# SBUF byte addresses of the split operands in a two-layer fp32 encoder step

## The chip, the cores and the metric

The kernel runs on one core of one Trainium2 chip. The metric is the device time of one execution in microseconds (us), given as the median of several runs. A profile of one execution comes with it: for every instruction its engine, its start, its duration and what it waited for. Times of single instructions are in ns. The engines are PE (matrix multiply), PEld (the weight loads that go with it), DVE, ACT and POOL (element work) and SP, whose queue issues most of the DMAs.

## What is computed

One inference step of a small two-layer encoder, over 1024 new rows and 64 rows of a running stream (1088 columns in the kernel, which works on transposed data). Cut to what matters here:

```python
def swiglu(u, w_in, w_out):
    g, up = jnp.split(u @ w_in, 2, axis=-1)
    return (jax.nn.silu(g) * up) @ w_out

def reference(...):
    for layer in range(2):
        nw = norm_w[layer]
        if layer == 0:
            mp, hp, cp = ssd_mixer(rmsnorm(xp, nw[0]), h0, c0, *params)
            ms, hs, cs = ssd_mixer(rmsnorm(xs, nw[0]), state_ssm[0], state_conv[0], *params)
        else:
            kp, vp = shared_kv(xp, kv_norm_w, w_kv)
            ks, vs = shared_kv(xs, kv_norm_w, w_kv)
            mp = prompt_band_attention((rmsnorm(xp, nw[0]) @ w_q), kp, vp, rel_bias) @ w_o
            ms = sample_band_attention((rmsnorm(xs, nw[0]) @ w_q), ks, vs, cache_k, cache_v, rel_bias) @ w_o
        xp = xp + rmsnorm(mp, nw[1])
        xs = xs + rmsnorm(ms, nw[1])
        xp = xp + rmsnorm(swiglu(rmsnorm(xp, nw[2]), ffn_w_in[layer], ffn_w_out[layer]), nw[3])
        xs = xs + rmsnorm(swiglu(rmsnorm(xs, nw[2]), ffn_w_in[layer], ffn_w_out[layer]), nw[3])
```

Model width is 1024, the hidden width of the feed-forward part 2816 (22 tiles of 128), the mixer's inner width 2048. Everything is float32.

## The kernel before, in words

**Split products.** Every large matrix product is made of three PE matmuls. Both operands are split into a high part, rounded to PE's `float32r` type, and the rest: weights into `h` and `l_`, activations into `xh` and `xl`. The three products are `h*xh`, `h*xl` and `l_*xh` (lines 458 to 460 in `passes`, 1304 to 1306 in `run_pair`, 1503 to 1505 in the second feed-forward product). In each matmul the weights, 128 by 128, are loaded into PE and stay there while the activations, 128 rows by 256 to 384 columns, stream past them. The weights are loaded anew for each matmul.

**Tiles in SBUF.** A tile is a block of bytes that has the same address in all 128 partitions. The tiles that this case is about:

- `r`, 16 tiles of 4608 bytes in pool `rp`: split activations of the mixer and of the attention, and in the feed-forward part those of the second half of the columns.
- `rx`, 13 tiles of 4096 bytes in pools `rx0` and `rx1`, one pool for each layer's back part: split activations of the first 512 columns, later part of the hidden activations; some are lent as landing places for weights from DRAM (`Lent`).
- `hl`, 3 tiles of 8192 bytes: the split weights. `hx`, 2 more of them at the start of each back part. `half` (split) and `tt` (unsplit): parts of weights for the seven-product scheme of `run_pair`.
- `raw`: weights as they come from DRAM. `sg`: landing places for hidden activations. `p1`, `u2`, `u3`, `c22`, `x` in pool `tm`: results of `run_pair` on their way to the gate.

Activations in `r` and `rx` lie there in blocks of 256, 288, 320 or 384 columns of 4 bytes, weights in blocks of 128 columns. All of these are multiples of 128 bytes, so each operand of a split matmul begins at the same byte in 128 as its tile.

**Order.** PE's instructions are recorded in the order of the code (`manual_schedule`); the class `Stream` puts side tasks between them by a clock of its own. The other engines are ordered by a scheduler with priorities. `Weights` loads and splits weights ahead of their use: DMA into `raw` or a lent `rx` tile, ACT rounds to the high part (line 340), DVE subtracts (line 341).

**Stages on the profile's time axis.** Mixer up to about 640 us; its output projection (`project`, 256 and 288 columns) to about 850; back part of layer 0, with `plain_pairs` (256 columns) to 920, `run_pair` (256 columns from `rx`, 288 from `r`) to 1327 and the second product (384, 384 and 320 columns) to about 1570; attention to about 2075; its output projection; and from about 2200 the back part of layer 1, built in the same way.

**Where addresses come from.** Pools are laid out one behind the other in the order in which they are opened, tiles in a pool likewise, each rounded up to 32 bytes. So the byte at which a tile begins follows from the sizes of all that lie before it.

Of the kernel before, what the change touches and what calls it, by code (L numbers as in the profile page):

```python
# [8 lines left out]
F32 = mybir.dt.float32  # L9
# [7 lines left out]
P = 128  # L17
# [120 lines left out]
class Ring:  # L138
# [9 lines left out]
    def get(self):  # L148
        assert self.free(), self.tag
        self.live += 1  # L150
        return self.pool.tile(self.shape, self.dtype, tag=self.tag, bufs=self.bufs, name=self.tag)
# [55 lines left out]
class Lent:  # L207
# [7 lines left out]

    def get(self):
        self.live += 1
        return self.ring.get()

    def put(self):  # L220
        self.live -= 1
# [153 lines left out]
def hybrid_kernel(  # L375
# [9 lines left out]
    def pool(es, name, bufs=1, **kw):  # L385
        return es.enter_context(tc.tile_pool(reuse_waits="tile", name=name, bufs=bufs, **kw))

    cp = pool(ctx, "cp")
    dr = ctx.enter_context(tc.tile_pool(name="dr", bufs=1, space=DRAM))
    wp = pool(ctx, "wp")  # L390
    rp = pool(ctx, "rp")
    nsb = pool(ctx, "nsb")
    pmm = pool(ctx, "pmm", 2, space=PSUM)
    pax = pool(ctx, "pax", 2, space=PSUM)
# [20 lines left out]
    yTv = yT_o.rearrange("(t p) n -> p t n", p=P)  # L415

    R = Ring(rp, "r", NR, [P, 1152])
    RX = Ring(None, "rx", 0, [P, 1024])
    W = Weights(
        nc, Ring(wp, "raw", RAWB, [P, 1024]), Ring(wp, "hl", HLB, [P, 2, 1024], F32R),  # L420
        Ring(None, "half", 0, [P, 2, 512], F32R), Ring(None, "tt", 0, [P, 1024]),
    )
    W.tc, W.lent = tc, Lent(RX)
    W.raws.append(W.lent)
# [13 lines left out]
    def ax(name):  # L438
        if side[0] and name in ("nst", "nbp"):
            return side[0].tile([P, 512], F32, tag="yy", name=name)  # L440
        return pax.tile([P, 512], F32, tag="ax", name=name)
# [44 lines left out]
    def rstd(ssum, inv, r, nb, more=None):  # L486

        sp = ax("nst")
        if more is None:
            for i in range(nb):  # L490
                PE.transpose(sp[:, i * P:(i + 1) * P], ssum[:, i * P:(i + 1) * P], ident)
        else:
            for j, t in enumerate((ssum, more)):
                for i in range(nb):
                    c = 4 * j + i
                    PE.matmul(sp[:, c:c + 1], t[:, i * P:(i + 1) * P], ones[:, 0:1], start=True, stop=True)
        with tc.high_priority(HIP):
            v = nsb.tile([P, 12], F32, tag="nv", bufs=2, name="nv")
            a, h, y = v[:, 0:nb], v[:, 4:4 + nb], v[:, 8:8 + nb]
            if more is None:  # L500
                sums = sp[:, :nb * P].rearrange("p (a b) -> p a b", b=P)
                V.tensor_reduce(a, sums, axis=mybir.AxisListType.X, op=ALU.add)
                V.tensor_scalar(a, a, inv, EPS, op0=ALU.mult, op1=ALU.add)
            else:
                V.tensor_scalar(a, sp[:, :nb], inv, EPS, op0=ALU.mult, op1=ALU.add)
                V.scalar_tensor_tensor(a, sp[:, 4:4 + nb], inv, a, op0=ALU.mult, op1=ALU.add)
            V.tensor_scalar(y.bitcast(I32), a.bitcast(I32), -0.5, float(0x5F3759DF), op0=ALU.mult, op1=ALU.add)


            V.tensor_tensor(h, y, y, op=ALU.mult)  # L510
            V.tensor_tensor(h, h, a, op=ALU.mult)
            V.scalar_tensor_tensor(a, h, RP[0], h, op0=ALU.add, op1=ALU.mult)
            V.scalar_tensor_tensor(a, a, RP[1], h, op0=ALU.add, op1=ALU.mult)
            V.scalar_tensor_tensor(a, a, RP[2], h, op0=ALU.add, op1=ALU.mult)
            V.scalar_tensor_tensor(r, a, RP[3], y, op0=ALU.add, op1=ALU.mult)

    def bcast(r, a, n, rb=None):

        bp = ax("nbp")
        for i in range((a + n + P - 1) // P):  # L520
            PE.transpose(bp[:, i * P:(i + 1) * P], r[:, i:i + 1].to_broadcast([P, P]), ident)
        if rb is None:
            rb = nsb.tile([P, 384], F32, tag="rb", bufs=1, name="rb")
        A.activation(rb[:, :n], bp[:, a:a + n], AF.Copy, scale=RL)
        return rb[:, :n]

    def rb_steps(ssum, n, out, wait=None, rb=None, more=None):

        nb = (n + P - 1) // P
        nr = nsb.tile([P, 4], F32, tag="nr", bufs=2, name="nr")  # L530
        rstd(ssum, 1.0 / D, nr[:, :nb], nb, more)
        yield 0.3, wait or RB_WAIT
        with tc.high_priority(HIP):
            out.append(bcast(nr, 0, n, rb))
        yield 0.35, 0
# [121 lines left out]
    with ExitStack() as es:  # L657
# [413 lines left out]
        for s in range(NSL):  # L1071
            us, n = u[s], SL[s][1]
            pl, tg = pyy, "yy"
# [68 lines left out]
    def op_build(ops, done, when=lambda: True):  # L1142


        n, qa, qb = ops.n, 2 * ops.b, 2 * ops.b + 1
        rings = (RX, R) if ops.b == 0 else (R,)
        L, rg = {}, {}
# [64 lines left out]
    def chain(layer, q, y, ss, cw, xsrc, xout, cpre, done):  # L1212

        o, n = QS[q]

        rings = (RX, R) if q < 2 else (R,)
        w_post, w_rb, w_pre = CHW[layer][q // 2]
# [43 lines left out]
    def plain_pairs(ts, ops, hd, px, tmp):  # L1261

        n = ops.n
        first = ts == PGS[0]
        xs, ws = {}, {}
        for t_, i, q in [(t_, i, q) for t_ in ts for i, q in (((0, 0), (1, 0), (0, 1), (1, 1)) if first else ((0, 0), (0, 1), (1, 0), (1, 1)))]:
            if (t_, i) not in ws:
                ws[t_, i] = W.get()
            st.wait_for(lambda: all(a_ in ops.plain for a_ in (f"a{q + 1}1", f"a{q + 1}2")))
            uq = ops.plain[f"a{q + 1}1"] + ops.plain[f"a{q + 1}2"]  # L1270
            if i == 0:
                xs[t_, q] = tmp.tile([P, n], F32, tag=("p1", "u3")[q] + f"{t_ % 2}", name="x")
            x = xs[t_, q]

            def gate(ps):
                with tc.high_priority(HIP):
                    A.activation(x, ps[:, :n], AF.Silu)

            def mult(ps):
                with tc.high_priority(HIP):  # L1280
                    V.tensor_tensor(x, ps[:, :n], x, op=ALU.mult)  # L1281
                nc.sync.dma_start(hd[:, t_, q * n:(q + 1) * n], x)

            unit(ws[t_, i], uq, n, mult if i else gate, pl=px)
            if q:
                W.put()
# [58 lines left out]
    def back(layer, start, cpost, xsrc, xmid, cpre, cpost2, xout, rb_out, done2):  # L1345
# [3 lines left out]
        with ExitStack() as es:  # L1349
            px = pool(es, f"px{layer}", 4, space=PSUM)  # L1350
            RX.pool, RX.bufs = pool(es, f"rx{layer}"), NRX
            sgp = pool(es, f"sg{layer}")
            stage[0] = lambda: sgp.tile([P, 384], F32, tag="sg", bufs=SGB, name="sg")

            def loader():

                for s, (o, n) in enumerate(SL):
                    yield 0, 0, lambda: phase[0] > (s > 0)
                    cells = Cells(n, *(((RX, 99), (R, 8)), ((R, 9), (RX, 99)), ((RX, 99), (R, 3)))[s])
                    for k in range(FT):  # L1360
# [10 lines left out]
            def end_load(s):  # L1371
                o, n = SL[s]
                xc = Cells(n, (R, 99)) if s == 2 else Cells(n, (RX, 99), (R, 99))
                yield 0, EP_W[s] if s < 2 else 0, lambda: xc.room(KD)
# [78 lines left out]
            with ExitStack() as e2:  # L1453
                tmp = pool(e2, f"tm{layer}")
                e3 = ExitStack()
                W.hx.pool, W.hx.bufs = pool(e3, f"hx{layer}"), 2
                W.advance()
                ops[0].yring, ops[1].yring = RX, R
                start(ops, px, lambda q, y, ss: st.spawn(chain(layer, q, y, ss, cpost, xsrc, xmid, cpre, dn)), dn)
                for ts in PGS:  # L1460
                    if ts == PGS[1]:
                        W.hx.bufs = 0
                    elif ts == PGS[-1]:
                        assert W.hx.live == 0
                        e3.close()
                        W.tt.pool, W.tt.bufs = pool(e2, f"tt{layer}"), 2
                        W.half.pool, W.half.bufs = W.tt.pool, 2

                        W.pri = HIP
                        W.advance()  # L1470
                    plain_pairs(ts, ops[0], hd, px, tmp)
                for r in ops[0].rings["a21"]:
                    r.put()
                for t_, bs, ends in [(t_, (0, 1), (0,) if t_ == FT - 1 else ()) for t_ in range(NB0, FT)] + [(t_, (1,), (1,) if t_ == NB0 - 1 else ()) for t_ in range(NB0)]:
                    run_pair(t_, W.get(), bs, ends, ops, hd, px, tmp, t_ == NB0)
                    W.pri = 0
                    if t_ == FT - 1:
                        phase[0] = 1
                        W.lent.cap = 2
                        st.spawn(loader())  # L1480
                W.tt.bufs = W.half.bufs = 0
# [5 lines left out]
            for s, (o, n) in enumerate(SL):  # L1487
# [3 lines left out]
                for m in range(KD):  # L1491
# [3 lines left out]
                    for k0, nk in KCH:  # L1495
                        w = W.get()
                        h, v = w["w"]
# [47 lines left out]
    rba = [rbp.tile([P, 384], F32, tag=f"rbf{s}", name="rbf") for s in range(NSL)]  # L1545
    done2 = []
    back(0, start_ssd, nwc(0, 1), xTv, x1d, nwc(0, 2), nwc(0, 3), x2d, rba, done2)


# [384 lines left out]
    def start_att(ops, px, after, dn):  # L1934
# [14 lines left out]
        st.spawn(op_build(ops[1], dn))  # L1949

    back(1, start_att, nwc(1, 1), x2d, x3d, nwc(1, 2), nwc(1, 3), yTv, None, [])
    st.flush()
    yY.close()
# [96 lines left out]
```

## Time and profile before

| what | value |
|---|---|
| median of 3 runs | 2952.55 us (2948.33 to 2952.82) |
| the profiled execution's own time | 2953.14 us |
| its span, first to last instruction | 2951.4 us |
| granted PE clock over the span | 0.997 |
| instructions | 56260, of them 21562 matmuls |

How to read it: the span is the stretch between the first and the last instruction; the 1.7 us between it and the execution's own time lie around it. In the groups of the profile a matmul's row names its line, the PSUM tile it writes, the tiles that it reads (`mmx<-r,hl` reads an `r` and an `hl` tile), the shape of the streamed operand, the count, the sum in us and the mean in ns. Matmuls are pipelined: the next one starts long before the one before has ended, so the mean duration is longer than the distance from start to start. `mm` and `mmx` are the PSUM tiles of `unit`, `px` those of `run_pair`, `po` that of the second feed-forward product.

### The profile page before, as it was taken

What the parts mean: (1) busy time and instruction counts of PE and PEld (TensorE: products, weight loads), DVE (VectorE), ACT (ScalarE), POOL (GpSimd) and SP (SyncE); (2) the same over time, 40 slices, a digit from 0 to 9 for tenths busy, and PEclk for the clock granted to TensorE, in tenths of its full rate; (3) what the DMA queues carried; (4) which work ended last, traced back from release to release, by engine and by line L of the source; (5) the groups of instructions that cost most, each with busy time, mean ns of one, the idle gap of its engine ahead of it and who ended that gap; (6) DMA issues with size and microseconds to landing.
All of it is one profiled execution on the core that took longest, in us unless ns stands there. A gap on an engine that the chain in (4) does not pass through costs nothing.

```text
span 2951.4 us, 56260 instructions
## 1 busy us (share of the span) xinstructions
PE 2911.9 (99%) x21562; PEld 2871.3 (97%) x21562; DVE 2032.0 (69%) x4452; ACT 1402.8 (48%) x2531; POOL 728.2 (25%) x884
## 2 busy tenths in 40 slices
PE   8999999999999999999999999999999999999999
PEld 8999999999999999999999899999999999999999
DVE  7887878885867545583567787778688555575544
ACT  6655546454443222353445665556664322244443
POOL 1333333331022434351111000000131434351111
PEclk9999999999999999999999999999999999999999
DMA  4333333335564222345665322223375222245754
GB/s 138 124 99 100 109 100 106 100 120 164 158 191 118 76 84 73 108 152 163 205 190 158 88 79 71 64 69 105 127 201 173 78 84 72 83 151 173 226 172 136
DMA packets 202846, 368.07 MB, mean 125 GB/s; under 512 B 20688, under 2 KB 149424, under 8 KB 202576
## 3 DMA queue, kind: packets, MB, share of 16 engines
q1 hardware_dynamic: 199920, 354.97, 38.3%
q0 software_dynamic: 2656, 9.51, 1.8%
q8 instruction: 169, 2.77, 0.4%
q14 instruction: 101, 0.83, 0.1%
HBM read 297.19 MB, written 62.74 MB: 122 GB/s over the span
## 4 chain that ended last, share of the span: by engine, by line
PE 86%; DVE 7%; DMA 3%; ACT 2%; issue 1%; POOL 0%; SPq 0%; DVEq 0%; ACTq 0%; POOLq 0%
PE px L1304 9%; PE px L1305 9%; PE px L1306 9%; PE mm L458 7%; PE mm L460 7%; PE mm L459 7%; PE po L1504 6%; PE po L1505 6%; PE po L1503 6%; PE mmx L460 3%; PE mmx L459 3%; PE mmx L458 3%; PE ptp L1736 2%; PE po L1771 2%; PE S L1705 1%
## 5 line engine op out<-in xcount | busy, mean ns | idle before, releaser
L458 PE MATMUL mm<-r,hl 128*128 128x384 f32 (+2 forms) x1704 | 565.5, 332 | 3.2 <-DVE craw L740 1.0
L460 PE MATMUL mm<-r,hl 128*128 128x384 f32 (+2 forms) x1704 | 549.9, 323 | 4.3 <-DVE hl L353 2.9
L459 PE MATMUL mm<-r,hl 128*128 128x384 f32 (+2 forms) x1704 | 548.5, 322 | 0.0
L341 DVE TENSOR_TENSOR hl<-raw,hl 128x1024 fp32r<-128x1024 f32 x216 | 255.6, 1184 | 217.8 <-ACT hl L340 215.6
L1305 PE MATMUL px<-r,hl 128*128 128x288 f32 (+1 forms) x1184 | 347.3, 293 | 0.0
L458 PEld LDWEIGHTS mm<-r,hl 128*128 128x128 f32 x1704 | 322.2, 189 | 6.0 <-DVE craw L740 1.1
L460 PEld LDWEIGHTS mm<-r,hl 128*128 128x128 f32 x1704 | 321.5, 189 | 6.2 <-DVE hl L353 4.2
L459 PEld LDWEIGHTS mm<-r,hl 128*128 128x128 f32 x1704 | 322.2, 189 | 0.3
L1304 PE MATMUL px<-r,hl 128*128 128x288 f32 x1056 | 311.0, 295 | 0.0
L1306 PE MATMUL px<-r,hl 128*128 128x288 f32 x1056 | 310.7, 294 | 0.0
L340 ACT CAST hl<-raw 128x1024 fp32r<-128x1024 f32 x216 | 216.9, 1004 | 161.5 <-PE po L1505 102.3
L484 POOL TENSOR_TENSOR ssum<-ssum,sq 128x256 f32<-128x256 f32 (+3 forms) x97 | 127.1, 1311 | 617.3 <-ACT sq L483 601.9
L1305 PEld LDWEIGHTS px<-r,hl 128*128 128x128 f32 x1184 | 222.3, 188 | 0.0
L1306 PE MATMUL px<-rx,hl 128*128 128x256 f32 x768 | 215.0, 280 | 5.2 <-DVE hl L341 5.2
L1304 PE MATMUL px<-rx,hl 128*128 128x256 f32 x768 | 215.6, 281 | 1.7 <-DVE x L1281 1.7
L1504 PE MATMUL po<-rx,hl 128*128 128x384 f32 (+1 forms) x624 | 201.7, 323 | 0.7 <-DVE rx L1368 0.7
L1304 PEld LDWEIGHTS px<-r,hl 128*128 128x128 f32 x1056 | 198.4, 188 | 0.4 <-DVE u L1319 0.4
L1306 PEld LDWEIGHTS px<-r,hl 128*128 128x128 f32 x1056 | 198.3, 188 | 0.0
L1503 PE MATMUL po<-rx,hl 128*128 128x384 f32 (+1 forms) x608 | 197.3, 324 | 0.0
L1505 PE MATMUL po<-rx,hl 128*128 128x384 f32 (+1 forms) x608 | 196.5, 323 | 0.0
L1305 PE MATMUL px<-rx,hl 128*128 128x256 f32 x640 | 178.8, 279 | 0.0
L1306 PEld LDWEIGHTS px<-rx,hl 128*128 128x128 f32 x768 | 145.3, 189 | 5.9 <-DVE hl L341 5.9
(364 smaller groups left out, 7921.7 us busy)
## 6 DMA issues: line engine op xcount, KB each, us to landing
raw<-in_w_f_dram SPq DMA_DIRECT2D x154, 512.0 KB, 3.8
rx<-in_w_f_dram SPq DMA_DIRECT2D x54, 512.0 KB, 3.6
raw<-in_w_in_dram SPq DMA_DIRECT2D x40, 512.0 KB, 3.6
MT<-ascr SPq DMA_DIRECT2D x48, 384.0 KB, 4.3
sg<-hscr SPq DMA_DIRECT2D x88, 192.0 KB, 3.6
raw<-in_w_f_dram SPq DMA_DIRECT2D x44, 384.0 KB, 3.3
raw<-in_w_so_dram SPq DMA_DIRECT2D x32, 512.0 KB, 3.8
raw<-in_w_o_dram SPq DMA_DIRECT2D x19, 512.0 KB, 3.7
```

The costliest lines, as they stand in the source:

```text
L340: self.nc.scalar.copy(h, v)
L341: (eng or self.eng or self.nc.vector).tensor_tensor(lo, v, h, op=ALU.subtract)
L458: PE.matmul(ps[:, :n], h_, xh, start=(first and i == 0), stop=False)
L459: PE.matmul(ps[:, :n], h_, xl, start=False, stop=False)
L460: PE.matmul(ps[:, :n], l_, xh, start=False, stop=(last and i == nk - 1))
L484: (eng or G).tensor_tensor(ssum[:, :n], ssum[:, :n], q[:, :n], op=ALU.add)
L1304: PE.matmul(ps, wh, ah[:, k, :], start=(k == 0), stop=False)
L1305: PE.matmul(ps, wh, al[:, k, :], start=False, stop=False)
L1306: PE.matmul(ps, wl, ah[:, k, :], start=False, stop=(k == 3))
L1503: PE.matmul(ps[:, :n], wh, xh, start=(k == 0), stop=False)
L1504: PE.matmul(ps[:, :n], wh, xl, start=False, stop=False)
L1505: PE.matmul(ps[:, :n], wl, xh, start=False, stop=(k == FT - 1))
```

## The change

No instruction is added, removed or moved: on all five engines the sequences of instructions are the same but for the numbers of buffers. Of the waits two differ: one ACT copy of 256 columns into an `rx` tile waits for one more DMA queue, and one POOL memset of a `K` tile no longer waits for PE. What changes is where tiles lie:

```diff
     def get(self):
         self.live += 1
-        return self.ring.get()
+        return self.ring.get()[:, :1024]
...
     wp = pool(ctx, "wp")
+    nss = pool(ctx, "nss")
     rp = pool(ctx, "rp")
+
+    def shift(pl):
+        pl.tile([P, 16], F32, name="shift")
+
     nsb = pool(ctx, "nsb")
...
-    RX = Ring(None, "rx", 0, [P, 1024])
+    RX = Ring(None, "rx", 0, [P, 1028])
...
-            v = nsb.tile([P, 12], F32, tag="nv", bufs=2, name="nv")
+            v = nss.tile([P, 12], F32, tag="nv", bufs=2, name="nv")
...
-        nr = nsb.tile([P, 4], F32, tag="nr", bufs=2, name="nr")
+        nr = nss.tile([P, 4], F32, tag="nr", bufs=2, name="nr")
...
                 W.hx.pool, W.hx.bufs = pool(e3, f"hx{layer}"), 2
+                shift(W.hx.pool)
...
                         W.tt.pool, W.tt.bufs = pool(e2, f"tt{layer}"), 2
+                        shift(W.tt.pool)
```

The small tiles `nv` and `nr` (192 bytes with rounding) move from behind `r` to a pool of their own ahead of it, so `r` begins 192 bytes later. The `rx` tiles grow by 16 bytes, which rounding makes 32. The first byte of each tile in 128, as the two programs are built:

| tile | before | after |
|---|---|---|
| `r` | 32 | 96 |
| `rx` | 96 | 96, 0, 32, 64 in turn |
| `hl`, `raw` | 32 | 32 |
| `hx`, `half`, `tt` | 96 | 64 |
| `sg`, tiles of pool `tm` | 96 | 0 |
| `ssum`, `sq` | 32 | 96 |
| tiles of the mixer and of the attention (`K`, `Qh`, `Ql`, `Vn` and others) | 64 or 96 | the same |

So the distance from the weights to the activations, (activations minus weights) in 128, changes as follows. The counts are split matmuls in the program.

| columns | activations on weights | matmuls | distance before | distance after |
|---|---|---|---|---|
| 256 | `r` on `hl` | 1364 | 0 | 64 |
| 256 | `r` on `hx` | 204 | 64 | 32 |
| 256 | `rx` on `hl` | 2860 | 64 | 64 (996), 96 (612), 0 (600), 32 (652) |
| 256 | `rx` on `half` | 384 | 0 | 64 (256), 96 (128) |
| 256 | `rx` on `hx` | 180 | 0 | 64 (60), 96 (40), 32 (60), 0 (20) |
| 288 | `r` on `hl` | 3792 | 0 | 64 |
| 288 | `r` on `half` and `hx` | 1056 | 64 | 32 |
| 320 | `r` on `hl` | 1760 | 0 | 64 |
| 320 | `rx` on `hl` | 832 | 64 | 64 (232), 96 (176), 0 (192), 32 (232) |
| 384 | `r` on `hl` | 4176 | 0 | 64 |
| 384 | `rx` on `hl` | 1008 | 64 | 64 (336), 96 (96), 0 (288), 32 (288) |

Of the 2860 matmuls of `rx` on `hl`, the 600 that come to distance 0 are 152 into `mmx` and 448 into `px`; the 1264 that come to 96 or 32 are 304 into `mmx` and 960 into `px`.

## The prediction

> **What bounds the kernel now.** I read the page first: busy time of each engine, then the chain that ended last.
>
> ```profile
> span 2951.4 us, 56260 instructions
> ...
> PE 2911.9 (99%) x21562; PEld 2871.3 (97%) x21562; DVE 2032.0 (69%) x4452; ACT 1402.8 (48%) x2531; POOL 728.2 (25%) x884
> ...
> PE 86%; DVE 7%; DMA 3%; ACT 2%; issue 1%; POOL 0%; SPq 0%; DVEq 0%; ACTq 0%; POOLq 0%
> ```
>
> PE is busy for 2911.9 of 2951.4 us and makes 86% of the chain. What PE saves or loses per matmul goes almost whole into the time, if addresses change a matmul at all. So I next read the groups by shape, for the same line and the same number of columns with other tiles.
>
> ```profile
> L458 PE MATMUL mmx<-rx,hl 128*128 128x256 f32 x228 | 64.4, 282 | 0.0
> L459 PE MATMUL mmx<-rx,hl 128*128 128x256 f32 x228 | 63.2, 277 | 0.0
> L460 PE MATMUL mmx<-rx,hl 128*128 128x256 f32 x228 | 63.1, 277 | 0.0
> L458 PE MATMUL mmx<-r,hl 128*128 128x256 f32 x220 | 62.5, 284 | 0.6 <-ACT r L602 0.6
> L460 PE MATMUL mmx<-r,hl 128*128 128x256 f32 x220 | 62.3, 283 | 1.1 <-DVE hl L341 1.1
> ...
> L459 PE MATMUL mmx<-r,hl 128*128 128x256 f32 x220 | 62.2, 283 | 0.5 <-DVE r L603 0.5
> ...
> L459 PE MATMUL mmx<-r,hx 128*128 128x256 f32 x68 | 18.8, 277 | 0.0
> ...
> L459 PE MATMUL mmx<-rx,hx 128*128 128x256 f32 x60 | 17.0, 283 | 0.0
> ...
> L1706 PE MATMUL S<-K,Ql 128*128 128x256 f32 x16 | 4.2, 280 | 0.0
> ```
>
> Set beside the table of distances: `rx` on `hl` and `r` on `hx`, distance 64, take 277. `r` on `hl` and `rx` on `hx`, distance 0, take 283. Each activation tile and each weight tile stands once on either side, so neither `r` nor `hx` is slow by itself; the pair is. `K` on `Ql`, distance 0 too, has 280. These durations hold a pipeline latency, so I checked the starts in the timeline (columns: start in us, duration), in a steady stretch of each.
>
> ```profile
> 2135.24 0.28 PE L460 MATMUL mmx<-r,hl 128*128 128x256 f32 x1
> ...
> 2136.92 0.28 PE L459 MATMUL mmx<-r,hl 128*128 128x256 f32 x1
> ```
>
> ```profile
> 2256.78 0.28 PE L460 MATMUL mmx<-rx,hl 128*128 128x256 f32 x1
> ...
> 2257.57 0.28 PE L458 MATMUL mmx<-rx,hl 128*128 128x256 f32 x1
> ```
>
> 14 steps in 1.68 us are 120 ns from start to start at distance 0; 7 steps in 0.79 us are 113 at distance 64. The difference is really time on PE. With more columns there is none:
>
> ```profile
> L1305 PE MATMUL px<-r,hl 128*128 128x288 f32 x1056 | 311.4, 295 | 0.0
> ...
> L1504 PE MATMUL po<-r,hl 128*128 128x384 f32 x368 | 123.1, 335 | 0.0
> ...
> L1504 PE MATMUL po<-rx,hl 128*128 128x384 f32 x336 | 112.6, 335 | 0.0
> ...
> L1505 PE MATMUL po<-rx,hl 128*128 128x320 f32 x272 | 83.9, 308 | 0.0
> ...
> L1305 PE MATMUL px<-r,half 128*128 128x288 f32 x176 | 51.9, 295 | 0.0
> ...
> L1505 PE MATMUL po<-r,hl 128*128 128x320 f32 x80 | 24.7, 309 | 0.0
> ...
> L1706 PE MATMUL S<-K,Ql 128*128 128x512 f32 x16 | 6.3, 392 | 0.0
> ```
>
> At 288 columns distance 0 and 64 both take 295, at 384 both 335, at 320 it is 309 against 308. The weight loads tell why:
>
> ```profile
> L459 PEld LDWEIGHTS mmx<-rx,hl 128*128 128x128 f32 x228 | 42.9, 188 | 0.0
> ...
> L459 PEld LDWEIGHTS mmx<-rx,hx 128*128 128x128 f32 x60 | 11.5, 191 | 0.0
> L746 PEld LDWEIGHTS dtp<-r,dtw 128*64 128x64 f32 x24 | 3.2, 135 | 0.7
> ```
>
> A load of 64 weight columns takes 135, one of 128 takes 188: 53 for 64 columns, so about 107 of the 188 are reading. That is nearly the whole 113 of a 256-column matmul: there the load of the next weights sets the pace, and at distance 0 it is itself longer (191). A stream of 288 columns or more outlasts the load and hides it.
>
> **The change part by part.** Prices are per matmul, distance 0 against 64, at 256 columns.
>
> In `mm` and `mmx` the means of the three lines give 283.3 against 278.7, so 4.7; the steady starts give 7. I take 6. In `px` the pieces are short and alternate with 288 columns:
>
> ```profile
> L1304 PE MATMUL px<-rx,hl 128*128 128x256 f32 x768 | 215.6, 281 | 1.7 <-DVE x L1281 1.7
> L1306 PE MATMUL px<-rx,hl 128*128 128x256 f32 x768 | 215.0, 280 | 5.2 <-DVE hl L341 5.2
> L1305 PE MATMUL px<-rx,hl 128*128 128x256 f32 x640 | 178.8, 279 | 0.0
> ...
> L1304 PE MATMUL px<-rx,half 128*128 128x256 f32 x128 | 36.2, 283 | 0.8 <-DVE p L1321 0.8
> L1306 PE MATMUL px<-rx,half 128*128 128x256 f32 x128 | 36.2, 283 | 0.0
> L1305 PE MATMUL px<-rx,half 128*128 128x256 f32 x128 | 36.1, 282 | 0.0
> ```
>
> 282.7 against 280: 2.7.
>
> `r` to byte 96. 1364 matmuls on `hl` go from distance 0 to 64, a pairing of bytes (96 on 32) that `rx` on `hl` has now: 1364 x 6 ns = 8.2 us less. The 9728 of 288, 320 and 384 columns on `hl` go the same way; the rows above say 0 within 1 ns, so nothing, with 5 us either way if half of that ns is real.
>
> `rx` in turn. 600 on `hl` come to distance 0: 152 x 6 + 448 x 2.7 = 2.1 us more. On `half` and `hx`, now at byte 64, 256 x 2.7 + 60 x 6 = 1.1 us less.
>
> The distances 32 and 96 have no row at 256 columns. Bounds: like 64, the 128 + 100 matmuls that leave distance 0 save 128 x 2.7 + 100 x 6 = 0.9 us and all others stay; like 0, the 960 + 304 of `rx` on `hl` and 204 of `r` on `hx` cost 960 x 2.7 + 508 x 6 = 5.6 us. The nearest row is `dtw` (byte 64, 384 columns from byte 32, distance 96):
>
> ```profile
> L746 PE MATMUL dtp<-r,dtw 128*64 128x384 f32 x16 | 5.4, 339 | 0.0
> ```
>
> 339 against 335, but with 64 weight columns. I take the end that is like 64, since only equal bytes show a cost, and keep the other for the range.
>
> The other engines read and write these tiles too:
>
> ```profile
> L341 DVE TENSOR_TENSOR hl<-raw,hl 128x1024 fp32r<-128x1024 f32 x172 | 213.5, 1242 | 162.0 <-ACT hl L340 159.8 <-DMA r<-x1d 2.0
> ...
> L340 ACT CAST hl<-raw 128x1024 fp32r<-128x1024 f32 x172 | 180.1, 1047 | 161.5 <-PE po L1505 102.3 <-PE px L1306 32.4 <-PE mm L460 8.1
> ...
> L341 DVE TENSOR_TENSOR hl<-rx,hl 128x1024 fp32r<-128x1024 f32 x50 | 62.0, 1240 | 82.1 <-ACT hl L340 82.1
> ...
> L340 ACT CAST hl<-rx 128x1024 fp32r<-128x1024 f32 x50 | 52.4, 1049 | 87.0 <-PE po L1505 72.9 <-PE px L1306 10.1 <-DVE nv L513 2.3
> ```
>
> From `raw` at byte 32 and from `rx` at byte 96 DVE takes 1242 and 1240, ACT 1047 and 1049: nothing. What a DMA into the new bytes costs is not shown, but weights are loaded ahead. The extra wait stands before one of 2531 ACT instructions: nothing, or a few us once if that DMA queue were late. Whether the others keep up with a faster PE:
>
> ```profile
> 850.00:920.00 70.00, 70.00 (x605) 70.00 (x604) 53.63 (x105) 29.91 (x42) 9.16 (x11) 1.00 0.75 214
> ...
> 2199.00:2268.00 69.00, 69.00 (x598) 69.00 (x597) 58.42 (x108) 31.43 (x43) 11.58 (x11) 1.00 0.79 224
> ```
>
> In these windows (length, then PE, PEld, DVE, ACT, POOL busy) of 256-column work PE never rests, and DVE, the next, has 11 to 16 us free. A few us from PE don't bring it to the bound.
>
> **Sum:** -8.2 + 2.1 - 1.1 - 0.9 = -8.1 us against the profiled 2953.14, so 2945.0. The median of the runs is 0.6 below that execution: 2944.5. With 4.7 for the price and 32 and 96 like 0 it comes to about 2953, with 7 to 2942; its own range is 2941 to 2953.
>
> [...]
>
> **Rivals.** First, a larger gain by the start of the stream itself. 320 to 384 columns cost 335 - 309 = 26, or 0.41 a column. By that rate 256 to 288 should cost 13 and costs 18 (277 to 295), 384 to 512 should cost 52 and costs 57 (335 to 392): a step of 5 to 6 behind each 128 columns or so. All streams now start at 32 or 96. If the step comes from starting 32 bytes off a multiple of 64, `rx` at 0 and 64 loses it: 1264 x 6 ns at 256 columns and two steps, 12 ns, for 792 of 320 and 384, 17 us more: 2927. For it: the steps. Against: nothing shows a stream that starts elsewhere.
>
> Second, no effect: 283 and 277 come from what runs beside those stages, not from bytes. 2952.5. Against it: the crossed pairs `r` on `hx` and `rx` on `hx`.
>
> Third, slower. If the load's reads run some ns behind those of the stream, the worst distance is 32 or 96 and not 0. If these cost twice the price of 0, that is (304 + 204) x 12 + 960 x 5.4 = 11.3 us, and the 228 that leave 0 lose 0.9 instead of gaining; with -8.2 + 2.1 - 1.1 it makes 5.0. The load then also outlasts 288 columns, where 1056 matmuls of `r` on `half` and `hx` pay another 6.3 us: +11.3, 2964. It decides as soon as the new distances cost more than 7.2 us together. For it: 339 against 335 on `dtw`. Against: at 64 columns of weights that row is no like case.
>
> **How the numbers follow.** Forecast 0.50, larger gain 0.20, no effect 0.12, slower 0.18. About 0.2% (6 us) is what a measurement of this kernel can tell from no change. Of the forecast's half, 0.08 falls within it. Faster: 0.42 + 0.20 = 0.62; same: 0.08 + 0.12 = 0.20; slower 0.18. The range takes the larger gain at the low end and the milder part of the slower case at the high end: 2926 to 2958.
>
> **What would show it.** In the profile after: `mmx<-r,hl` at 256 columns down from 283 to 277 on lines 459 and 460; `px<-rx,half` down toward 281; `px<-rx,hl` at 256 up by some 0.5 on average if 32 and 96 are like 64, by 1.7 if they are like 0 (448 or 1408 of 2176, 2.7 each). The 384 and 320 rows of `po<-rx,hl` unchanged; if they fall by several ns the first rival holds. Loads of `half` and `hx` at 288 columns above 188 speak for the third. DVE and ACT rows unchanged. Wrong would be a change in 288 to 384 columns of `r` on `hl` of more than 1 ns: 9728 matmuls would outweigh every other term.

## The result: 7 us slower, where 8 us less was forecast

| | before | after |
|---|---|---|
| median of 8 runs each, us | 2950.98 | 2958.40 |
| lowest to highest, us | 2948.33 to 2953.26 | 2956.14 to 2960.95 |
| profiled execution, us | 2953.14 | 2956.14 |
| its span, us | 2951.4 | 2954.4 |

The ratio after to before is 1.0028, its 95% interval 1.0018 to 1.0037: slower by 5 to 11 us. 2958.4 lies just above the range (2926 to 2958), on the side that had 18 chances of 100.

The two profiled executions lie only 3.0 us apart. That of before stands 2.2 us above the median of its runs, that of after is the fastest of its own. The spacing of PE's starts shows where the rest is. I set each matmul's start-to-start time beside that of the same matmul before (21562 on either side, in the same order). Those that changed by under 60 ns sum to +8.2 us. The 75 others sum to -5.3 us. Of these, 42 (-1.6 us) lie in stretches of 3.4 us in which the granted clock was 0.5, of which before has one more (at 97 us); 33 (-3.7 us) are steps around waits, which in all ten experiments with the whole model, too, sum to 1 to 4 us less than in this one profile of before. So the sums below leave both out. On the page of after, again the busy times and the chain:

```profile
span 2954.4 us, 56261 instructions
...
PE 2917.6 (99%) x21562; PEld 2878.5 (97%) x21562; DVE 2029.2 (69%) x4452; ACT 1401.6 (47%) x2531; POOL 724.7 (25%) x884
...
PE 87%; DVE 6%; DMA 3%; ACT 2%; issue 1%; POOL 0%; SPq 0%; DVEq 0%; ACTq 0%; POOLq 0%
```

PE is busy 5.7 us longer for the same 21562 matmuls; DVE, ACT and POOL are a little shorter. The one instruction more is a wait on ACT's queue. The matmuls themselves take longer. Which ones, the groups by shape of after say (busy us, mean ns of one, then idle time; every line number here is 5 to 7 higher than before). Two of before, which stood at 335 and 295:

```profile
L459 PE MATMUL mm<-r,hl 128*128 128x384 f32 x1008 | 338.1, 335 | 0.0
...
L459 PE MATMUL mmx<-r,hx 128*128 128x288 f32 x176 | 51.9, 295 | 0.0
```

And of after:

```profile
L464 PE MATMUL mm<-r,hl 128*128 128x384 f32 x1008 | 339.3, 337 | 0.0
L1310 PE MATMUL px<-r,hl 128*128 128x288 f32 x1056 | 311.7, 295 | 0.0
L1311 PE MATMUL px<-rx,hl 128*128 128x256 f32 x768 | 216.8, 282 | 4.6 <-DVE hl L341 4.6
L1309 PE MATMUL px<-rx,hl 128*128 128x256 f32 x768 | 216.4, 282 | 1.2 <-DVE x L1286 1.2
L1310 PE MATMUL px<-rx,hl 128*128 128x256 f32 x640 | 180.7, 282 | 0.0
L1511 PE MATMUL po<-r,hl 128*128 128x384 f32 x368 | 124.1, 337 | 0.0
...
L1511 PE MATMUL po<-rx,hl 128*128 128x384 f32 x336 | 113.4, 337 | 0.0
...
L465 PE MATMUL mmx<-rx,hl 128*128 128x256 f32 x228 | 64.0, 281 | 0.0
L464 PE MATMUL mmx<-rx,hl 128*128 128x256 f32 x228 | 63.8, 280 | 0.0
...
L464 PE MATMUL mmx<-r,hl 128*128 128x256 f32 x220 | 61.5, 279 | 0.6 <-DVE r L608 0.6
L465 PE MATMUL mmx<-r,hl 128*128 128x256 f32 x220 | 61.5, 279 | 1.1 <-DVE hl L341 1.1
...
L464 PE MATMUL mmx<-r,hx 128*128 128x288 f32 x176 | 52.5, 298 | 0.0
...
L1310 PE MATMUL px<-r,half 128*128 128x288 f32 x176 | 52.6, 299 | 0.0
...
L1311 PE MATMUL px<-rx,half 128*128 128x256 f32 x128 | 36.0, 281 | 0.0
```

`r` on `hl` at 256 columns fell from 283 to 279, most of what was forecast. Against it `rx` on `hl` rose from 277 to 280 or 281 in `mmx` and from 280 to 282 in `px`, `mm` and `po` at 384 columns from 335 to 337, and `r` on `half` and `hx` at 288, on the lines shown, from 295 to 298 or 299.

Where the words below say "step", it is the mean time from one matmul's start to the next, worked out from the starts in the trace, steps with a wait left out. A rhythm is a step that a stretch of back-to-back matmuls keeps. Set against the forecast, sums in us over the matmuls of each kind:

| matmuls | forecast | after |
|---|---|---|
| `r` on `hl`, 256 columns | -8.2 | -5.2 |
| `rx` on `hl`, 256 | +2.1 | +7.5 |
| `r` and `rx` on `half` and `hx`, 256 | -2.0 | -0.4 |
| `r` on `half` and `hx`, 288 | 0 | +1.8 |
| `r` on `hl`, 288 | 0 | -1.5 |
| 320 and 384 | 0 | +6.3 |
| the rest | 0 | -0.2 |
| sum | -8.1 | +8.2 |

The 6.3 us at 320 and 384 are 5.8 at 384 columns (4.2 of them in `po`) and 0.5 at 320.

### The profile page after: what moved, and what is told of

Same layout as the page of the kernel before. It is cut to its first block, busy times and chain, and to the rows that moved or that the text cites. A ratio compares the mean times of both kernels' runs of the same rounds, so it can differ in the third digit from the quotient of the medians.

```text
span 2954.4 us, 56261 instructions
## 1 busy us (share of the span) xinstructions
PE 2917.6 (99%) x21562; PEld 2878.5 (97%) x21562; DVE 2029.2 (69%) x4452; ACT 1401.6 (47%) x2531; POOL 724.7 (25%) x884
## 4 chain that ended last, share of the span: by engine, by line
PE 87%; DVE 6%; DMA 3%; ACT 2%; issue 1%; POOL 0%; SPq 0%; DVEq 0%; ACTq 0%; POOLq 0%
PE px L1310 9%; PE px L1311 9%; PE px L1309 9%; PE mm L463 8%; PE mm L465 8%; PE mm L464 8%; PE po L1511 6%; PE po L1512 6%; PE po L1510 6%; PE mmx L464 3%; PE mmx L465 3%; PE mmx L463 3%; PE ptp L1743 2%; PE po L1778 2%; PE S L1712 1%
```

## Experiments

Twelve kernels, of which ten are the whole model with other first bytes, and two are PE alone. In diffs `nss`, `shift` and the wider `rx` are those of the change. Base is the kernel before, unless another is named.

**`r` alone.** The new pool moves `r` from 32 to 96; `rx`, `half` and `hx` stay at 96.

```
     wp = pool(ctx, "wp")
+    nss = pool(ctx, "nss")
     rp = pool(ctx, "rp")
...
-            v = nsb.tile([P, 12], F32, tag="nv", bufs=2, name="nv")
+            v = nss.tile([P, 12], F32, tag="nv", bufs=2, name="nv")
...
-        nr = nsb.tile([P, 4], F32, tag="nr", bufs=2, name="nr")
+        nr = nss.tile([P, 4], F32, tag="nr", bufs=2, name="nr")
```

> r at byte 96 alone; rx stays at 96, hx and half at 96. Pair theory (a matmul's cost is set by the distance in 128 between its own stream and the weights): mmx<-r,hl at 256 columns goes from 283 to 277, r on hl at 288, 320 and 384 columns stays at 295, 309 and 334, r on half and hx comes to distance 0; time 6 to 8 us below before. Rhythm theory (equal starts one after the other run in a cheap rhythm, changing starts break it, also for the matmuls behind them): all starts are equal within r and within rx, so po<-r,hl at 384 columns stays at 334 and the time falls by 5 to 8 us. Theory that byte 96 in r is dear at 384 columns by itself: po<-r,hl at 338 as with the whole change, and a time only 0 to 4 us below before.

Measured: 1.0000 (0.9991 to 1.0009). Two rows of this kernel's groups by shape:

```profile
L460 PE MATMUL mmx<-r,hl 128*128 128x256 f32 x220 | 61.5, 279 | 0.9 <-DVE r L604 0.9
...
L1505 PE MATMUL po<-r,hl 128*128 128x384 f32 x368 | 123.7, 336 | 0.0
```

The gain at 256 columns is there, 5.2 us by the steps, and is given back: 4.1 at 384 columns, 1.7 by `r` on `half` and `hx`, which now has distance 0. One of the terms at 384 is `po<-rx,hl`: its step went from 173.3 to 174.7 ns although neither `rx` nor `hl` moved. So neither the pair theory nor the rhythm theory has the time (5 to 8 us less), and the third, which put `po<-r,hl` at 338 for its own byte, doesn't explain the pair that did not move.

**The turn of `rx` alone.**

```
-        return self.ring.get()
+        return self.ring.get()[:, :1024]
...
-    RX = Ring(None, "rx", 0, [P, 1024])
+    RX = Ring(None, "rx", 0, [P, 1028])
...
             sgp = pool(es, f"sg{layer}")
+            sgp.tile([P, 24], F32, name="shift")
```

> rx at 96, 0, 32 and 64 in turn alone; r stays at 32, hx, half, sg and the tiles of tm at 96. Pair theory: only rows of rx rise, px<-rx,hl at 256 columns from 280 to 282, po<-rx,hl by 1 to 2, po<-r,hl at 384 columns stays at 334; time 5 to 9 us above before. Rhythm theory: po<-r,hl at 384 columns rises to about 338 too, though its tiles have not moved; time 9 to 15 us above before.

Measured: 1.0016 (1.0007 to 1.0025), 4.7 us slower. In the groups by shape:

```profile
L1305 PE MATMUL px<-rx,hl 128*128 128x256 f32 x640 | 180.1, 281 | 0.0
L1505 PE MATMUL po<-r,hl 128*128 128x384 f32 x368 | 123.0, 334 | 0.0
...
L1505 PE MATMUL po<-rx,hl 128*128 128x384 f32 x336 | 113.2, 337 | 0.0
```

`po<-rx,hl` pays, `po<-r,hl` beside it doesn't: the rows of the pair theory, at a time just under its range. By the steps `rx` on `hl` at 256 columns costs 6.8 us, at 384 another 1.4. By the timed medians this edit alone makes over half of the loss.

**`half`, `hx` and `tt` alone, to 64.**

```
                 W.hx.pool, W.hx.bufs = pool(e3, f"hx{layer}"), 2
+                W.hx.pool.tile([P, 24], F32, name="shift")
...
                         W.tt.pool, W.tt.bufs = pool(e2, f"tt{layer}"), 2
+                        W.tt.pool.tile([P, 24], F32, name="shift")
```

> hx, half and tt at byte 64 alone; r at 32, rx at 96. r on them is then at distance 96, rx on them at 32. Pair theory: rx on half and hx fall from 283 to 277 if 32 is as good as 64, and stay if it is like 0; r on half and hx at 288 columns stays at 295 or rises by 2 as in the whole change; time within 2 us of before. Rhythm theory: the same, no other row moves.

Measured: 0.9990 (0.9981 to 0.9999), about 3 us less. The moved pairs gave 0.4 at 256 columns and lost 0.3 at 288; 2.0 came from `rx` on `hl`, which did not move (the `px` step went from 116.0 to 115.0). So a pair's step can change without its bytes.

**The change without the turn**: the first and the third together, `rx` at 96.

> The whole change without the wider rx tiles: r at 96, hx, half and tt at 64, rx all at 96, sg and tm at 96. If the turn of rx carries the loss, the time is within 3 us of before and po<-rx,hl at 384 columns at or below 335; r on half and hx at 288 columns, distance 32, rises from 295 to 296 or 297 and costs 1.5 to 2 us. If it is the three parts together in a way that none shows alone, the time is 4 to 8 us above before.

Measured: 0.9994 (0.9986 to 1.0003). Without the wider `rx` the change costs nothing that can be told. Only `po<-rx,hl`, expected at or below 335, has 336 and 337.

**Every stream at 96 and every weight at 32.** The first experiment's edit, and the third's with 16 for 24, so that all pairs have distance 64 and nothing takes turns.

> r at 96, rx at 96, hx, half and tt at 32: every large split matmul streams from byte 96 on weights at byte 32, distance 64. Pair theory as corrected by the pairs measured alone: 256 columns of r on hl at about 115 from start to start and of rx on half and hx at about 116, 288 at 132.3; 3 to 6 us below before, if 384 columns stay at 173.5; the rhythm theory lets 384 columns fall into 175 to 177 in some stretches, as with r at 96 alone, which gives 2 to 4 us back: then 0 to 4 us below.

Measured: 0.9972 (0.9960 to 0.9984), some 8 us below before, more than the 3 to 6 expected; it beats both kernels. Its groups by shape:

```profile
L1306 PE MATMUL px<-rx,hl 128*128 128x256 f32 x640 | 179.6, 281 | 0.0
...
L1507 PE MATMUL po<-r,hl 128*128 128x384 f32 x368 | 123.6, 336 | 0.0
...
L460 PE MATMUL mmx<-rx,hl 128*128 128x256 f32 x228 | 63.2, 277 | 0.0
...
L460 PE MATMUL mmx<-r,hl 128*128 128x256 f32 x220 | 61.1, 278 | 0.6 <-DVE r L604 0.5
...
L1306 PE MATMUL px<-rx,half 128*128 128x256 f32 x128 | 35.7, 279 | 0.0
...
L460 PE MATMUL mmx<-r,hx 128*128 128x256 f32 x68 | 18.8, 276 | 0.0
...
L460 PE MATMUL mmx<-rx,hx 128*128 128x256 f32 x60 | 16.6, 277 | 0.0
```

In `mmx` all four pairs, on the lines shown, now stand at 276 to 278, whichever tile; 384 columns still cost 336, not 334.

**`rx` at 64 throughout**, without turns, `r` and the weights as before.

```
             RX.pool, RX.bufs = pool(es, f"rx{layer}"), NRX
+            RX.pool.tile([P, 24], F32, name="shift")
             sgp = pool(es, f"sg{layer}")
+            sgp.tile([P, 8], F32, name="shift")
```

> rx all at byte 64, equal starts, r at 32, weights as before: distance 32 on hl, 96 on half and hx. If the bytes cost and not the turn: px<-rx,hl and mmx<-rx,hl at 256 columns from 280 and 277 to 282 to 284 (starts 118 to 120 apart), 2860 x 3 to 4 ns, so 8 to 12 us above before, more than with the tiles in turn. If changing starts are what costs: as before, within 2 us.

Measured: 1.0013 (1.0005 to 1.0022), some 4 us, between what the two theories gave. The byte itself counts at 256 columns (`rx` on `hl` +3.8 by the steps, all at distance 32 now). At 384 columns it hardly does: the step of `po<-rx,hl` is 173.6 ns against 173.3.

**The turn in other settings.** Three kernels add the second experiment's edit to others: to `r` alone, to the weights at 64, and to the fastest kernel; the fourth is the change again.

> r at 96 and rx in turn, hx, half, tt, sg and tm at 96. If the parts add up: 1.000 x 1.0016, 3 to 6 us above before. If r at 96 makes the turn dearer, because the changed starts of rx throw the stretches of r into a slower rhythm: po<-r,hl at 384 columns at 337 or more, time 7 to 11 us above.

> rx in turn and hx, half and tt at 64, r at 32. If the parts add up: 1.0016 x 0.999, 0 to 4 us above before, po<-r,hl at 384 columns at 334. If the weights at 64 make the turn dearer: 5 us or more above.

> The best version so far (r at 96, hx, half and tt at 32) with rx in turn, so the price of the turn alone in that setting. If it is that of e2_rx_turn: 0.9972 x 1.0016, 2 to 5 us below before. If r at 96 makes the turn dearer: within 2 us of before.

> The whole change again, beside the other combinations on the same chip: 1.0018 to 1.0037 of before. Rhythm theory: the rows of 384 columns, po<-r,hl and po<-rx,hl, stand at 336 to 338 again, since the entry into each stretch is the same program.

Measured, each ratio against the kernel before in the same session:

| setting | without the turn | with it | the turn adds |
|---|---|---|---|
| kernel before | 1 | 1.0016 (1.0007 to 1.0025) | 0.16% |
| `r` at 96 | 1.0000 (0.9991 to 1.0009) | 1.0026 (1.0015 to 1.0038) | 0.26% |
| weights at 64 | 0.9990 (0.9981 to 0.9999) | 1.0020 (1.0011 to 1.0029) | 0.30% |
| both (the change) | 0.9994 (0.9986 to 1.0003) | 1.0022 (1.0013 to 1.0031) | 0.28% |
| all pairs at 64 (the fastest) | 0.9972 (0.9960 to 0.9984) | 1.0018 (1.0010 to 1.0027) | 0.46% |

The turn costs 5 to 14 us wherever it is put. That it costs more where more is to be lost is what the sizes suggest, but each interval is about 0.1% to either side. `r` at 96 and the weights at 64 came out on the dearer branch of what was expected; the fastest kernel with the turn, 5 us above before, lies outside both (2 to 5 us below, or within 2). With `r` at 96 and the turn, `sg` and the tiles of `tm` are at 96 as before, so their move is not needed for the loss. In the last kernel `po<-r,hl` shows one part of it; neither `r` nor `hl` differs from the fastest kernel, which had 336:

```profile
L1507 PE MATMUL po<-r,hl 128*128 128x384 f32 x368 | 124.1, 337 | 0.0
```

The change again shows something else. One stretch of `mm<-r,hl` at 256 columns, 324 matmuls, runs differently in two executions of the same program. From its later part, the timeline of after, and then of the change again:

```profile
671.73 0.28 PE L465 MATMUL mm<-r,hl 128*128 128x256 f32 x1
...
690.77 0.28 PE L465 MATMUL mm<-r,hl 128*128 128x256 f32 x1
```

```profile
674.27 0.28 PE L465 MATMUL mm<-r,hl 128*128 128x256 f32 x1
...
693.35 0.28 PE L465 MATMUL mm<-r,hl 128*128 128x256 f32 x1
```

168 steps in 19.04 us are 113.3 each, 162 in 19.08 are 117.8, with the same bytes and a granted clock of 1.00 in both. By this and its neighbours `r` on `hl` at 256 gains 3.9 us in the second execution and 5.2 in the first. So the program alone does not fix the step.

**PE alone, 16 pairs of bytes.** The model is left out; blocks of 48 matmuls run back to back, with streams `xa` to `xd` at bytes 0, 32, 64, 96 and weights `wa` to `wd` likewise, in one order (`u`) and in the reverse (`v`).

```
+                h, l_ = Wt[w][:, k * P:(k + 1) * P], Wt[w][:, 1024 + k * P:1024 + (k + 1) * P]
+                xh, xl = X[a][:, k * n:(k + 1) * n], X[b][:, (8 + k) * n:(9 + k) * n]
+                PE.matmul(ps[:, :n], h, xh, start=(k == 0), stop=False)
+                PE.matmul(ps[:, :n], h, xl, start=False, stop=False)
+                PE.matmul(ps[:, :n], l_, xh, start=False, stop=(k == 7))
...
+    for n, a, w in ORD:
+        block("u", a, a, w, n)
+    for n, a, w in ORD[::-1]:
+        block("v", a, a, w, n)
```

> PE alone, the model is left out: units of 48 split matmuls, streams at byte 0, 32, 64, 96 (xa to xd) on weights at 0, 32, 64, 96 (wa to wd), 256, 288, 320 and 384 columns, once in this order (tile u) and once in the reverse order (v); then streams of two different bytes in turn on wb (m), each followed by xd on wb (t). Pair theory: at 256 columns 276 at distance 64 and 283 at 0 in both orders, t the same as u of xd on wb, 276 and at 384 columns 335. Rhythm theory: xd on wb differs between u, v and t by what ran before it, by 2 to 4 ns at 384 columns, and m is 2 to 6 above u. Start theory (the first rival of the prediction): xa and xc take 12 ns less than xb and xd at 320 and 384 columns whatever the weights.

Steps in ns, in the order `u`, over the second half of each block (0 on 0 at 256 columns, the first block, is left out):

| columns | lowest pair | highest pair | equal bytes |
|---|---|---|---|
| 256 | 113.3 (64 on 0) | 120.0 (four pairs) | 118.6 to 118.8 |
| 288 | 132.2 (eight pairs) | 134.5 (32 on 0) | 133.3 to 133.4 |
| 320 | 146.7 | 146.7 | 146.7 |
| 384 | 173.3 (five pairs) | 176.7 (five pairs) | 176.0 to 176.1 |

From 100 to 880 us of this run the profile has DVE, ACT and POOL busy for 0.00 us, a DMA share of 0.00 and a granted clock of 1.00, so these differences come from PE's own work. At 320 columns bytes do nothing, and streams from 0 and 64 are not faster as such: the rival of the larger gain falls. At 288 columns the distance sorts the pairs: 132.2 at 64 and 96, 133.3 or 133.4 at 0, 133.3 to 134.5 at 32. At 256 the pair 96 on 32, 113 in steady stretches of the kernel, has 117.8 here, but 113.3 in eleven of twelve blocks that follow a mix of two streams (the expectation's `t`). And at 384 all four pairs at distance 32 differ between the two orders, one of them so. The timeline, start and duration in us, first and last matmul of the block of `xa` on `wd`, in `u`:

```profile
340.19 0.34 PE L81 MATMUL u<-xa,wd 128*128 128x384 f32 x1
...
348.50 0.34 PE L83 MATMUL u<-xa,wd 128*128 128x384 f32 x1
```

and in `v`:

```profile
550.53 0.34 PE L81 MATMUL v<-xa,wd 128*128 128x384 f32 x1
...
558.67 0.33 PE L83 MATMUL v<-xa,wd 128*128 128x384 f32 x1
```

47 steps in 8.31 us are 176.8 each, 47 in 8.14 are 173.2.

**PE alone, one pair entered in different ways.** Here `xd` on `wb` (96 on 32) is run after pauses (`p`), after blocks that mix it with another stream (`l`, 288 matmuls) and after other widths (`q`).

```
+        for cols in (64, 128, 256, 384, 512, 640, 768, 896, 1024):
+            pause(cols)
+            block("p", "d", "d", "b", n)
+        for a in "abcd":
+            block("m", a, "d", "b", n)
+            block("l", "d", "d", "b", n, 12)
+        for o in (256, 288, 320, 384):
+            block("o", "d", "d", "b", o)
+            block("q", "d", "d", "b", n)
```

> PE alone, the model is left out: xd on wb, the same bytes throughout, entered in different ways: after pauses of different length (p), after units with a stream from another byte (l, 288 matmuls each), after units of other widths (q), and in a mix with 288 columns and with xa (f, g, h). Pair theory: one value, 113 from start to start at 256 columns and 173 at 384, whatever came before. Rhythm theory: each stretch settles at one of a few values (113.3 or 117.8 at 256; 173.3, 174.7 or 176.7 at 384), which depends on how it was entered, and keeps it to its end, also over 288 matmuls.

The timeline of this kernel, first and last rows of five steady pieces, all of the same two tiles:

```profile
89.81 0.28 PE L81 MATMUL l<-xd,wb 128*128 128x256 f32 x1
...
92.31 0.28 PE L82 MATMUL l<-xd,wb 128*128 128x256 f32 x1
...
261.83 0.28 PE L81 MATMUL q<-xd,wb 128*128 128x256 f32 x1
...
264.31 0.28 PE L81 MATMUL q<-xd,wb 128*128 128x256 f32 x1
...
289.80 0.34 PE L82 MATMUL p<-xd,wb 128*128 128x384 f32 x1
...
293.44 0.34 PE L82 MATMUL p<-xd,wb 128*128 128x384 f32 x1
...
369.83 0.34 PE L81 MATMUL l<-xd,wb 128*128 128x384 f32 x1
...
373.36 0.34 PE L83 MATMUL l<-xd,wb 128*128 128x384 f32 x1
...
425.76 0.34 PE L83 MATMUL l<-xd,wb 128*128 128x384 f32 x1
...
429.43 0.34 PE L83 MATMUL l<-xd,wb 128*128 128x384 f32 x1
```

At 256 columns 22 steps in 2.50 us are 113.6, and 21 in 2.48 are 118.1. At 384 columns 21 in 3.64 are 173.3, 20 in 3.53 are 176.5, 21 in 3.67 are 174.8. The durations (0.28, 0.34) hardly tell them apart. Each stretch keeps its value to its end, the `l` ones over 288 matmuls. 118 came after blocks of 288 and 320 columns, 176.5 after a mix with `xa`, 174.8 after mixes with `xb` and `xc`. Of the nine pauses at 384 columns seven were hidden: PE went on without a break, at 173.3. The two that held PE up (360 and 945 ns from start to start) were followed by 176.7. So this pair of bytes has not one step but two at 256 columns and three at 384, and which one a stretch keeps goes with what ran before it. Each of the two kernels was executed once.

## Why the prediction was wrong

The steps' sums in us against before, and the time as the ratio gives it (ratio less 1, times 2951):

| matmuls | after | `r` alone | turn alone | weights 64 | no turn | all at 64 | all at 64, turn | `rx` at 64 |
|---|---|---|---|---|---|---|---|---|
| `r` on `hl`, 256 | -5.2 | -5.2 | 0.0 | -0.1 | -6.2 | -5.4 | -5.0 | 0.1 |
| `rx` on `hl`, 256 | 7.5 | -0.5 | 6.8 | -2.0 | -0.1 | -1.3 | 7.8 | 3.8 |
| on `half`, `hx`, 256 | -0.4 | 0.8 | -0.7 | -0.4 | 0.0 | -2.8 | -1.2 | -0.1 |
| on `half`, `hx`, 288 | 1.8 | 0.6 | 0.0 | 0.3 | 0.9 | 0.1 | -0.2 | 0.2 |
| `r` on `hl`, 288 | -1.5 | -1.2 | -0.2 | 0.0 | -1.3 | -1.4 | -2.0 | 1.6 |
| 320 and 384 | 6.3 | 4.8 | 1.3 | 0.1 | 4.2 | 3.6 | 6.3 | 0.1 |
| sum with the rest | 8.2 | -1.0 | 7.1 | -2.3 | -2.7 | -7.2 | 5.8 | 5.4 |
| timed | 8.3 | 0.0 | 4.7 | -3.0 | -1.8 | -8.3 | 5.3 | 3.8 |

One profile each, and the sums follow the timed medians within 2.4 us. The three kernels that are not in the table have 9.8 for 7.7 timed (`r` at 96 and the turn), 7.1 for 5.9 (weights at 64 and the turn) and 9.4 for 6.5 (the change again). To that accuracy the steps account for the time.

**What bounds the kernel** held: PE makes 87% of the chain, and the steps between its starts account for the loss.

**`r` to byte 96** was right in sign and place, -5.2 of -8.2 (-3.9 in the change again). The step in `mm` and `mmx` fell from 119.6 to 115.0, 4.6 ns and not the 6 that I chose between 4.7 and 7. 115.0 lies between the two steps, 113 and 118, that this pair has when PE runs alone.

**"I take the end that is like 64"** for distances 32 and 96 is the first step that failed. By first byte, `rx` on `hl` at 256 columns:

| byte of `rx` | matmuls | distance | step before | step after | costs, us |
|---|---|---|---|---|---|
| 96, not moved | 996 | 64 | 115.5 | 117.7 | 2.2 |
| 32 | 600 | 0 | 114.6 | 118.0 | 1.9 |
| 0 | 612 | 96 | 116.4 | 118.0 | 1.0 |
| 64 | 652 | 32 | 116.2 | 119.9 | 2.4 |

The costs add up to 7.5. The 600 at distance 0 cost 1.9 of the 2.1 that I gave them. The 1264 at 96 and 32, forecast at nothing, cost 3.4. The 996 that did not move, also forecast at nothing, cost 2.2. If each matmul is charged with the step before it and not the one behind it, the four rows are 1.6, 2.7, 1.2 and 1.8, so the split is rough and the sum is not. The end "like 0" (5.6 us with `r` on `hx`) stood in the text, and the trace had no row for either: I chose the cheap end for want of a row.

**One price for one pair** is the premise under all of it, and it fell. The 996 that did not move pay 2 ns each; the experiments on PE alone have two steps, 113 and 118, for just that pair, and so have the two executions of the changed program. With the turn alone the same `rx` tiles at the same bytes cost 2.3, 1.3, 1.7 and 1.4 us, in the order of the table. My rows of before, 277 and 283, were means over the rhythms that these stretches happened to be in, and I took them for the price of the bytes. The crossed pairs seemed to prove it. They proved that bytes matter, not that they alone do.

**"With more columns there is none"**, the 0 at 288, 320 and 384, is the other step that failed, and I had named it as what would outweigh the rest. 4176 + 1008 matmuls at 384 columns cost 5.8 us. Before, all of them stood at 173.3 to 174.3, so equal rows at distances 0 and 64 said "no effect" where they showed one rhythm out of three. With `r` alone at 96 `mm` rose by 0.5 ns and `po` to 174.7; the turn alone took `po<-rx,hl` to 174.8; both together have `po` at 175.1 and 175.8. At 288 columns `r` on `half` and `hx` took 1.8 us more and `r` on `hl` 1.5 less, which almost cancel.

**The cause that I gave**, a load of weights that is lengthened by the stream and sets the pace, isn't borne out. In before the loads of `mmx<-rx,hl` took 188, of `px<-r,half` (288 columns) 188 or 189. In after the matmuls are slower and the loads, to 1 ns, are as long as they were:

```profile
L464 PEld LDWEIGHTS mmx<-rx,hl 128*128 128x128 f32 x228 | 43.0, 189 | 0.0
L463 PEld LDWEIGHTS mmx<-rx,hl 128*128 128x128 f32 x228 | 42.9, 188 | 0.0
...
L1310 PEld LDWEIGHTS px<-r,half 128*128 128x128 f32 x176 | 33.1, 188 | 0.0
```

At 384 columns, too, the loads of `po` take 187 or 188 in both profiles, and the steps differ all the same. The 191 at distance 0 is a longer load beside a longer step; which of the two makes the other is not shown. The 107 of 188 that I counted as reading was my estimate from the loads of 64 and 128 weight columns (135 and 188); no run shows a load's reading by itself.

**`half` and `hx`**: `px<-rx,half` at 281 as forecast, but not the whole 2.0: -0.8 for `rx`, +0.4 for `r` on `hx` that came to distance 32.

**The other engines** hid their part: DVE 2029.2, ACT 1401.6, no new wait of weight.

**The rivals.** The larger gain by streams from 0 and 64 is refuted (320 columns: 146.7 for all sixteen pairs). No effect is refuted by the fastest kernel, 0.9960 to 0.9984 by addresses alone, and what runs beside PE is not needed for the difference: with PE alone at work the sixteen pairs take 113.3 to 120.0 at 256 columns. The slower case had the sign right, but not its way: the matmuls that came from distance 64 to 32 or 96 cost 5.6 us at 256 and 288 columns and 6.6 with 384, under the 7.2 that it needed. Its 288-column term had the place, 1.8 us and not 6.3. Its price didn't hold: `rx` on `hl` at 256 columns pays 1.6 ns at distance 96 and 3.7 at 32, not twice the 3.3 at distance 0, and 5.8 us at 384 columns were not in it. One end of the forecast's own range is added up wrongly by 1 us: with 7 ns it comes to 2943.

**Left open**: what the rhythms are, whether a read of PE waits in the slow ones, and why a mix, a block of another width or a hold-up is followed by one or the other. Also why `r` at 96 costs 384 columns something where `r` at 32 did not. The runs name the conditions and not the mechanism.

## What to carry to other kernels

When PE is back to back, it is worth trying one first byte in 128 for all streams and another for all weights (here 96 and 32: 0.28% less; no other such pair was tried in the whole kernel), and a ring whose tiles drift through several bytes is worth a look (here 5 to 14 us in five settings). A price that is read from a group of like matmuls belongs to their whole sequence (here 996 matmuls whose bytes stayed cost 2.2 us), so a layout is tried in the whole kernel, and a "no effect" at one width is checked at more than one pair of addresses (here 384 columns, alike at 173.3 to 174.3 before, cost 5.8 us). Where the profile has no row for a new case, the forecast should not rest on its cheap end.

## What was new about the hardware

- Back-to-back matmuls of the same tiles run at one of several stable steps: for a stream at byte 96 and weights at 32, 113 or 118 ns at 256 columns; 173, 175 or 177 at 384. A stretch keeps its step, over up to 288 matmuls.
- The first bytes of stream and weights change the step at 256 (113.3 to 120.0), 288 (132.2 to 134.5) and 384 columns (173.3 to 176.7) and not at 320, where all sixteen pairs take 146.7.
- Much of the rhythm comes again, not all: in the profile of the change and in that of its repetition the `po` steps agree within 0.1 ns (175.78 and 175.79; 175.12 twice), while one stretch of `mm<-r,hl` has 113.3 in one and 117.8 in the other.
